# X, B and C of an SSD layer as pairs of seven block products ahead of the scan, a decay matrix by one exponential and a predicated copy, and what is left of the filler tiles behind

## The chip, the cores and the metric

The kernel runs on one core of one Trainium2 chip. The metric is the device time of one execution in microseconds (us), the median of several runs.

## The reference

It is a two-layer encoder on a sequence of 1024 tokens with 1024 channels, all in float32. The change touches the first layer alone, whose core is this:

```
proj = x @ w_in
z, xbc, dt_raw, sc_bg, sc_cg, sc_h, sc_gate = split(proj)
xbc = silu(depthwise_conv4(xbc) + conv_b)
xs, bm, cm = split(xbc)                    # 16 heads of 64; 4 groups of B and C, 128 states each
y_a = ssd(xs, bm, cm, dt) + ssd(flipped)   # both directions, chunks of 128
y_a = rms_norm(y_a * silu(z))
y_b = sc_bg * conv3(sc_cg * sc_h) * silu(sc_gate)
out = concat([y_a, y_b]) @ w_out
```

In a chunk of the scan, with cs the running sum of dt*a:

```
cb     = einsum('bclgn,bcsgn->bcgls', cq, bq)
y_diag = einsum('bcgls,bcgrls,bcsgrp->bclgrp', cb, exp(masked difference of cs), xd)
states = einsum('bclgn,bcgrl,bclgrp->bcgrpn', bq, decay_states, xd)
y_off  = einsum('bclgn,bcgrpn,bcgrl->bclgrp', cq, h_in, exp(cs))
```

Then follows a layer norm, and a second layer with latent attention and pooling.

## The kernel before

Every weight and x is split into a high and a low part in fp32r, and each product is three matmuls (high by high, high by low, low by high). A weight tile is loaded by SyncE (SP) as 512 KB into a raw buffer (wraw, three of them), cast by ScalarE to whi, and VectorE makes wlo as the difference. An output tile of 128 channels by 1024 tokens (key X, B, C or br, PSUM tile gps, of which there are two) has 8 steps of 6 matmuls of 128x512. PSUM also has four tiles of 512 columns (pool pb) for all small products.

A function main_plan writes the order of the work as a list, and a scheduler with pools of buffers fixes each engine's order from it:

- z of group 0 (zdp, evicted as zx) and the time steps dt, then the tiles B, C, X0, X1 of group 0.
- For each of four groups g a second pass (op_p2: a chunk's transposes xps, its scaled xd, its states sps; for later groups z tiles beside them), then a third pass over 8 chunks. Its front part (op_p3f) makes cbp = B'C and the decay matrix E: both directions of a row of cs come from DRAM by a broadcast transfer (E2 from crow, four buffers), VectorE adds a mask of -1e30, ScalarE takes 8 exponentials with a bias eb for each head and direction, VectorE adds the two halves and multiplies by cbp. Its back part (op_p3b) makes yo (from the states) and yd (E by x), and VectorE, GpSimd and ScalarE gather them as ta and yg; yg goes to DRAM (yad).
- In each chunk of a third pass stand F3 = 6 steps of filler tiles: the 16 br tiles of the short convolution and the X, B, C tiles of the next group. br tiles come in fours: q=1 is copied (bru), q=2 multiplied by it and convolved (bra), q=0 multiplied in, q=3 is the gate, after which the tile is stored (ybd).
- Behind the scan, four tiles of combinations of x are made (op_tp: xtraw loaded, differences, split to xT), and the other 16 br tiles go as 8 pairs, each by seven block products of 12 matmuls (sA, sB, sD; op_sw prepares the weight combinations from sraw, op_sp does a product).

A wrapper named issue_after places the mask add of a third pass behind the second pass's sixth xd. Four buffers of E2 mean that a chunk's transfer waits for the yd four chunks earlier.

Of the kernel before, what the change touches and what calls it, by code (L numbers as in the profile page):

```python
# [18 lines left out]
P = 128  # L19
# [12 lines left out]
NEG = np.float32(-1e30)  # L32
# [32 lines left out]
F2, F3, FB, FC = 0, 6, 4, 0  # L65
J0 = 4
# [11 lines left out]
def main_plan():  # L78
# [6 lines left out]
    def to_front(keys):  # L85
        n = 0
        while n < len(queue) and queue[n][2] != 0:
            n += 1
        queue[n:n] = [s for key in keys for s in tile_steps(key)]

# [4 lines left out]
    for key in (("B", 0), ("C", 0), ("X", 0), ("X", 1)):  # L95
        queue += tile_steps(key)
    ops.append(("dt",))
    pull(len(queue))
    for j in range(J0):
        for q in BR_ORDER:  # L100
            queue += tile_steps(("br", q, j))
    for g in range(G):
        ops.append(("z0", g))
        pull(FB)
        for i, c in enumerate(C2):
# [3 lines left out]
            pull(F2)  # L109
# [9 lines left out]
        pull(FC)  # L119
        for i, c in enumerate(C3):  # L120
# [6 lines left out]
            pull(F3)  # L127
            ops.append(("p3b", g, c))
        while any(s[1][0] in ("B", "C", "X") for s in queue):
            pull(1)  # L130
# [5 lines left out]
    ops += [("sw", 0, i) for i in range(SW_N)]  # L136
    pull(len(queue))
    ops.append(("sw", 1, 0))
    for n in range(NP):
        for i in range(7):  # L140
            ops.append(("sp", n, i))
            if n + 1 < NP and 0 < i + 1 < SW_N:
                ops.append(("sw", n + 1, i + 1))
        if n + 2 < NP:
            ops.append(("sw", n + 2, 0))
        if n in YA_P:
            ops.append(("ya", YA_P.index(n)))
# [4 lines left out]

SW_N = 6
YA_P = (1, 2)
PAIRS = [p for j in range(J0, 8) for p in ((("br", 1, j), ("br", 2, j)), (("br", 3, j), ("br", 0, j)))]
# [28 lines left out]
def pack(inputs):  # L184
# [17 lines left out]
    consts = np.concatenate([ident, up, up.T, NEG * (1 - up), NEG * (1 - up.T)], axis=1)  # L202
# [47 lines left out]
class Weights:  # L250
    def __init__(self, k, pool, ahead=1):
        self.k, self.pool, self.ahead = k, pool, ahead
        self.seq, self.idx = weight_seq(), weight_index()
        self.limit = self.seq.index(("O", 0))
        self.loaded = self.done = self.used = 0
        self.raw, self.out = {}, {}
# [24 lines left out]
    def release(self):  # L281
        self.limit = len(self.seq)
        self.split(self.used + 1 + self.ahead)
# [13 lines left out]
def setup(k):  # L297
# [4 lines left out]
    cs = k.const.tile([P, 640], F32, name="consts")  # L302
    k.ident, k.up, k.lo = (cs[:, 128 * i:128 * i + 128] for i in range(3))
    k.mask = view(cs[:, 384:640], 2)
# [114 lines left out]
def dt_chain(k, tp, X):  # L419
    nc, a, sp = k.nc, k.a, k.dts_pool  # L420
    V = nc.vector
    alog = tp.tile([P, 32], F32, name="alog")
    nc.sync.dma_start(out=alog, in_=a["alog"].partition_broadcast(P))
    dsk = tp.tile([P, 32], F32, name="dsk")
# [18 lines left out]
    dt = t("dt")  # L443
    V.scalar_tensor_tensor(out=dt, in0=p, scalar=2.0, in1=X, op0=ALU.mult, op1=ALU.add)
    da = t("da")
    V.scalar_tensor_tensor(out=view(da, NB), in0=view(dt, NB), scalar=-1.0, in1=bc_mid(aexp, 1, NB), op0=ALU.mult, op1=ALU.mult)
    ones = tp.tile([P, P], F32, name="ones")
# [11 lines left out]
    k.eb = sp.tile([P, 256], F32, name="eb")  # L459
# [3 lines left out]
    dec = t("dec")  # L463
    V.tensor_tensor(out=dec, in0=cp[:, 256:512], in1=k.cs, op=ALU.subtract)
    nc.scalar.activation(out=dec, in_=dec, func=AF.Exp)
    V.tensor_scalar(out=dt, in0=dt, scalar1=0.25, scalar2=None, op0=ALU.mult)
    V.tensor_tensor(out=k.dw, in0=dec, in1=dt, op=ALU.mult)
    V.tensor_scalar(out=dt, in0=dt, scalar1=1e-37, scalar2=None, op0=ALU.max)
    nc.scalar.activation(out=dt, in_=dt, func=AF.Ln)
    V.tensor_tensor(out=k.eb, in0=dt, in1=k.cs, op=ALU.subtract)  # L470
    k.crow = k.dram.tile([NB, 2, 16 * P], F32, name="crow")
    rowT = big(k, "rowT").bitcast(F32)[:32, 0:NB * P].rearrange("p (c l) -> p c l", c=NB)
# [17 lines left out]
def layer0_main(k):  # L490
# [1077 lines left out]
```

## Time and profile before

| | |
|---|---|
| runs | 1423.72, 1423.87, 1426.09 us (median 1423.87) |
| profiled execution | 1426.95 us |
| its span | 1424.8 us |
| mean granted clock of TensorE | 0.997 |

The three runs and the profiled execution are of the same kernel; a span goes from the first to the last instruction. The first filler matmul (gps) starts at 35.06 us, the gate pairs at 555.33, and the output projection of the first layer at 712.40.

### The profile page before, as it was taken

How to read it: one execution, taken by the hardware profiler on the slowest of the kernel's cores; microseconds unless marked ns; L12 is line 12 of the kernel's file. 1: busy time of each engine (PE TensorE's matmuls, PEld its weight loads, DVE VectorE, ACT ScalarE, POOL GpSimd, SP SyncE). 2: the span in 40 equal slices, each digit the busy share in tenths (PEclk: the TensorE clock that was granted, in tenths of full speed). 3: DMA queues.
4: the chain of work that ended last, by engine and by line, in shares of the span. 5: the costliest groups of instructions: out<-in, count | busy, mean ns of one | idle time of the engine just before them, and what ended most of it. 6: DMA issues, size and time to landing. Idle time of an engine off the chain costs nothing.

```text
span 1424.8 us, 19565 instructions
## 1 busy us (share of the span) xinstructions
PE 1394.6 (98%) x7287; PEld 1187.2 (83%) x7287; DVE 931.3 (65%) x1512; ACT 655.7 (46%) x1301; POOL 478.7 (34%) x443
## 2 busy tenths in 40 slices
PE   8999999999999999999999999999999999999997
PEld 8887798888889787788888888898888888988886
DVE  5758858839965947866564543733327888888485
ACT  5446545537536423433243422522225888878410
POOL 0013635423733543433210430612310445546210
PEclk9999999999999999999999999999999999999999
DMA  7221523421430524232268355211100000001232
GB/s 253 69 72 45 119 75 91 109 82 32 144 114 10 150 82 140 80 95 74 85 196 274 104 159 192 81 32 45 44 23 1 1 1 1 1 31 60 89 118 89
DMA packets 47726, 123.39 MB, mean 87 GB/s; under 512 B 5512, under 2 KB 10384, under 8 KB 47632
## 3 DMA queue, kind: packets, MB, share of 16 engines
q1 hardware_dynamic: 47632, 122.14, 27.8%
q8 instruction: 58, 0.95, 0.3%
q14 instruction: 36, 0.29, 0.1%
HBM read 105.21 MB, written 16.91 MB: 86 GB/s over the span
## 4 chain that ended last, share of the span: by engine, by line
PE 79%; DVE 10%; DMA 3%; ACT 3%; issue 2%; POOL 2%; DVEq 0%; SPq 0%; ACTq 0%; POOLq 0%
PE sA L907 6%; PE gps L409 5%; PE gps L410 5%; PE gps L412 5%; PE ops L412 4%; PE ops L410 4%; PE ops L409 4%; PE tps L1390 3%; PE fps L404 3%; PE fps L402 3%; PE fps L403 3%; PE sD L907 3%; PE sps L402 2%; PE sps L403 2%; PE sps L404 2%
## 5 line engine op out<-in xcount | busy, mean ns | idle before, releaser
L409 PE MATMUL gps<-x,whi 128*128 128x512 f32 x512 | 206.2, 403 | 3.6 <-DVE cacc L593 3.0
L410 PE MATMUL gps<-x,whi 128*128 128x512 f32 x512 | 202.3, 395 | 0.0
L412 PE MATMUL gps<-x,wlo 128*128 128x512 f32 x512 | 162.8, 396 | 0.1
L484 DVE TENSOR_TENSOR wlo<-wraw,whi 128x1024 fp32r<-128x1024 f32 x66 | 85.4, 1297 | 76.7 <-ACT whi L483 76.5
L483 ACT CAST whi<-wraw 128x1024 fp32r<-128x1024 f32 x66 | 69.0, 1049 | 122.7 <-PE ops L412 38.6
L409 PEld LDWEIGHTS gps<-x,whi 128*128 128x128 f32 x512 | 96.7, 189 | 26.4 <-issue 3.1
L412 PEld LDWEIGHTS gps<-x,wlo 128*128 128x128 f32 x512 | 95.7, 189 | 21.2 <-issue 1.2
L410 PEld LDWEIGHTS gps<-x,whi 128*128 128x128 f32 x512 | 96.7, 189 | 19.7 <-issue 1.2
L1376 POOL TENSOR_SCALAR pt<-pt,sm 128x1024 f32<-128x1024 f32 x64 | 72.8, 1138 | 114.3 <-DVE sm L1375 63.3
L484 POOL TENSOR_TENSOR xdl<-xd,xdh 128x512 fp32r<-128x512 f32 (+1 forms) x32 | 40.2, 1256 | 178.7 <-ACT xdh L483 175.3
L484 DVE TENSOR_TENSOR PT<-tps,PT 128x512 fp32r<-128x512 f32 x128 | 84.1, 682 | 14.2 <-ACT PT L483 14.0
L771 ACT ACTIVATE E<-E,eb 128x128 f32<-128x128 f32 x256 | 78.4, 391 | 25.3 <-DVE E L768 17.9
L1370 DVE TENSOR_REDUCE nm<-sps 128x1 f32<-128x1024 f32 x64 | 77.9, 1218 | 9.5 <-PE sps L404 9.3
L987 POOL TENSOR_TENSOR rs<-rs,neghalf 128x1 f32<-128x1 f32 x16 | 12.9, 811 | 210.5 <-DVE nm L1022 142.8
L1374 ACT ACTIVATE pt<-sps,nm 128x1024 f32<-128x1024 f32 x64 | 71.8, 1122 | 17.4 <-DVE nm L1371 12.6
L483 ACT CAST PT<-tps 128x512 fp32r<-128x512 f32 x128 | 70.0, 588 | 17.2 <-PE tps L1390 16.6
L795 POOL TENSOR_TENSOR ta<-to,ta 128x256 f32<-128x256 f32 x56 | 57.5, 1027 | 53.0 <-DVE to L788 50.1
L402 PE MATMUL fps<-x1hi,whi 128*128 128x512 f32 x192 | 74.9, 390 | 0.0
L404 PE MATMUL fps<-x1hi,wlo 128*128 128x512 f32 x192 | 74.7, 389 | 0.0
L403 PE MATMUL fps<-x1lo,whi 128*128 128x512 f32 x192 | 74.7, 389 | 0.0
L593 DVE SCALAR_TENSOR_TENSOR cacc<-gps,vec,cacc 128x512 f32<-128x512 f32 (+1 forms) x96 | 71.5, 745 | 2.4 <-ACT cacc L589 1.4
L1390 PE MATMUL tps<-consts,pt 128*128 128x128 f32 x512 | 70.9, 274 | 0.6 <-DVE PT L484 0.3
(372 smaller groups left out, 3823.9 us busy)
## 6 DMA issues: line engine op xcount, KB each, us to landing
wraw<-in_wt_dram SPq DMA_DIRECT2D x82, 512.0 KB, 4.3
E<-crow SPq DMA_DIRECT2D x32, 512.0 KB, 5.6
sraw<-in_wt_dram SPq DMA_DIRECT2D x16, 512.0 KB, 4.3
yad<-yg SPq DMA_DIRECT2D x32, 128.0 KB, 2.2
ybd<-bra SPq DMA_DIRECT2D x16, 256.0 KB, 2.4
xtraw<-in_xT_dram SPq DMA_DIRECT2D x8, 512.0 KB, 3.8
yab<-yad SPq DMA_DIRECT2D x8, 512.0 KB, 3.5
ybr<-ybd SPq DMA_DIRECT2D x8, 512.0 KB, 4.4
```

Source lines behind the costliest of these rows:

```text
L402: nc.tensor.matmul(out, shi, mhi, start=start, stop=False)
L403: nc.tensor.matmul(out, shi, mlo, start=False, stop=False)
L404: nc.tensor.matmul(out, slo, mhi, start=False, stop=stop)
L409: nc.tensor.matmul(out, shi, mhi, start=start, stop=False)
L410: nc.tensor.matmul(out, shi, mlo, start=False, stop=False)
L412: nc.tensor.matmul(out, slo, mhi, start=False, stop=stop)
L483: nc.scalar.copy(out=hi, in_=src)
L484: lo_eng.tensor_tensor(out=lo, in0=src, in1=hi.bitcast(F32), op=ALU.subtract)
L771: A.activation(out=E4[:, d, h], in_=E4[:, d, h], func=AF.Exp, bias=eb4[:, c, d, 4 * g + h:4 * g + h + 1])
L907: PE.matmul(ps, s_[:, kk, :], x_, start=fresh and kk == 0 and m == 0, stop=kk == 3 and m == 2, skip_group_check=True)
L1370: V.tensor_reduce(out=nm, in_=ps, axis=AX.X, op=ALU.max)
L1390: PE.transpose(out=ps[:, P * c:P * c + P], in_=pt[:, P * (4 * h + c):P * (4 * h + c) + P], identity=k.ident)
```

## The change

- X, B and C are no filler tiles any more. They become 8 pairs, (B, C) and (X, X) of each group, by the same seven block products as the gate pairs, all ahead of the scan. Each result is convolved over 1024 columns at a time, with one Silu, stored to DRAM (xbd), and loaded again for its group by op_xl.
- The combinations xT are made in front, under the first 4 br tiles, and again behind for the gate pairs. z of group 0 goes by DRAM too (z0d).
- The other 12 br tiles (96 steps) are the filler: 8 steps ahead of the scan, 1 a chunk in group 0's second pass, and 3, 2, 2 and 3 a chunk in the third passes.
- The decay matrix: the backward half gets a bias of ed (the difference of the two biases), a mask is copied into PSUM, a predicated copy puts the backward half over the forward one, and then there is one set of four exponentials. What both directions count on the diagonal goes into cd, which takes dsum's place in ta.

```diff
-F2, F3, FB, FC = 0, 6, 4, 0
-J0 = 4
+F2, F3, FB, FX = (1, 0, 0, 0), (3, 2, 2, 3), 0, 8
+JF, J0 = 1, 4
...
+    per = len(queue) // 4
+    for t in range(4):
+        pull(per // 2)
+        ops.append(("tp", t))
+        if t == 3:
+            ops.append(("sw", 0, 0))
+        pull(per - per // 2)
+    pull(len(queue))
+    ops += [("sw", 0, i) for i in range(1, SW_N)]
+    ops.append(("sw", 1, 0))
+    ops.append(("dt",))
+    pairs(0, NF, SW_FRONT, {})
+    for j in range(JF, J0):
+        for q in BR_ORDER:
+            queue += tile_steps(("br", q, j))
+    ops.append(("ssd",))
+    pull(FX)
...
         if g + 1 < G:
-            to_front([("X", 2 * g + 2), ("X", 2 * g + 3), ("B", g + 1), ("C", g + 1)])
+            ops.append(("xl", g + 1))
...
+PAIRS = [p for g in range(G) for p in ((("B", g), ("C", g)), (("X", 2 * g), ("X", 2 * g + 1)))]
+NF = len(PAIRS)
...
+    def op_xl(g):
+        groups[g]["xfm"] = view(big(k, "xfm").bitcast(F32), 4)
+        for j in (2, 3, 0, 1):
+            nc.sync.dma_start(out=groups[g]["xfm"][:, j], in_=k.xbd[g, :, j])
...
+        acc = acc4("cacc")
+        A.activation(out=acc, in_=u, func=AF.Identity, bias=k.vec[:, V_CONVB + idx:V_CONVB + idx + 1], scale=w(2))
+        for i, sh in ((1, -1), (0, -2), (3, 1)):
+            a0, a1 = max(-sh, 0), S - max(sh, 0)
+            V.scalar_tensor_tensor(out=acc[:, a0:a1], in0=u[:, a0 + sh:a1 + sh], scalar=w(i), in1=acc[:, a0:a1], op0=ALU.mult, op1=ALU.add)
+        A.activation(out=acc, in_=acc, func=AF.Silu)
+        nc.sync.dma_start(out=k.xbd[g, :, j], in_=acc)
...
         with tc.issue_after(st["xd", C2[E_AT]]):
-            V.tensor_tensor(out=E4, in0=E4, in1=bc_mid(k.mask, 2, HPG), op=ALU.add)
+            for h in range(HPG):
+                A.activation(out=E4[:, 1, h], in_=E4[:, 1, h], func=AF.Identity, bias=ed4[:, c, 4 * g + h:4 * g + h + 1])
+            A.copy(out=later, in_=k.mask)
+            V.copy_predicated(out=E, mask=bc_mid(later.bitcast(I32), 1, HPG), data=E4[:, 1])
         for h in range(HPG):
-            for d in range(2):
-                A.activation(out=E4[:, d, h], in_=E4[:, d, h], func=AF.Exp, bias=eb4[:, c, d, 4 * g + h:4 * g + h + 1])
-        V.tensor_tensor(out=E, in0=E, in1=tb, op=ALU.add)
-        V.tensor_tensor(out=view(E, HPG), in0=view(E, HPG), in1=bc_mid(cbp, 1, HPG), op=ALU.mult)
+            A.activation(out=E[:, h], in_=E[:, h], func=AF.Exp, bias=eb4[:, c, 0, 4 * g + h:4 * g + h + 1])
+        cd = tp.tile([P, 8], F32, name="cd", tag="cd", bufs=3)
+        junk = tp.tile([P, P], F32, name="junk", tag="junk", bufs=1)
+        V.scalar_tensor_tensor(out=junk, in0=cb, scalar=1.0, in1=k.ident, op0=ALU.mult, op1=ALU.mult, accum_out=cd[:, 4:5])
+        V.scalar_tensor_tensor(out=cd[:, 0:4], in0=dt4[:, c, 1, g4], scalar=cd[:, 4:5], in1=k.dsum[:, g4], op0=ALU.mult, op1=ALU.add)
+        V.tensor_tensor(out=E, in0=E, in1=bc_mid(cb, 1, HPG), op=ALU.mult)
```

What this does to the order shows at three places. First VectorE at the start, with L859 the differences of op_tp, L573 and L577 the evictions of dt and z; in the kernel after:

```order
L495 TENSOR_TENSOR wlo_424<-wraw_376,whi_423 128x1024
L495 TENSOR_TENSOR wlo_494<-wraw_427,whi_493 128x1024
L859 TENSOR_TENSOR xtraw_454<-xtraw_454 128x512
L859 TENSOR_TENSOR xtraw_454<-xtraw_455,xtraw_454 128x512
L859 TENSOR_TENSOR xtraw_455<-xtraw_455,xtraw_454 128x512
L859 TENSOR_TENSOR xtraw_455<-xtraw_455 128x512
L495 TENSOR_TENSOR xT4_462<-xtraw_454,xT4_462 128x1024
L573 TENSOR_TENSOR dtx_380<-zdp_96,dtb_381 128x64
L573 TENSOR_TENSOR dtx_380<-zdp_97,dtb_381 128x64
L495 TENSOR_TENSOR xT4_462<-xtraw_455,xT4_462 128x1024
```

Before, the evictions (there L562 and L565) follow the two weight splits at once; now a tile of combinations stands between them.

Second, ScalarE at the end of group 1's third pass, in the kernel after. L794 is the addition of ed, L798 the exponentials, L831 the squares of a finished chunk; E2_3398 and E2_3447 belong to the last two chunks of group 1, E2_4018, E2_4037 and E2_4093 to the first three of group 2:

```order
L794 ACTIVATE E2_3447<-E2_3447,ed_786 128x128 x4
L795 COPY cbp_3396<-consts_63 128x128
L794 ACTIVATE E2_4018<-E2_4018,ed_786 128x128 x4
L798 ACTIVATE E2_3398<-E2_3398,dtx_380 128x128 x4
L795 COPY cbp_3445<-consts_63 128x128
L831 ACTIVATE ta_3387,ssq_67<-yg_3392 128x256
L794 ACTIVATE E2_4037<-E2_4037,ed_786 128x128 x4
L798 ACTIVATE E2_3447<-E2_3447,dtx_380 128x128 x4
L831 ACTIVATE ta_3436,ssq_67<-yg_3441 128x256
L794 ACTIVATE E2_4093<-E2_4093,ed_786 128x128 x4
```

The additions for group 2 stand between those of group 1 and its exponentials. In the kernel before, what first touches the next group's E2 (E2_2107 to E2_2291 of group 1) is VectorE's mask add, behind that group's sixth xd:

```order
L712 TENSOR_TENSOR xd_1938<-xps_1930,dw_448 128x512
L768 TENSOR_TENSOR E2_2107<-E2_2107,consts_63 128x1024
L768 TENSOR_TENSOR E2_2122<-E2_2122,consts_63 128x1024
L768 TENSOR_TENSOR E2_2198<-E2_2198,consts_63 128x1024
L768 TENSOR_TENSOR E2_2291<-E2_2291,consts_63 128x1024
```

The first touch of a new group's E2 has moved to another engine and from behind the second pass to ahead of the last exponentials of the group before.

Third, TensorE between the scan and the gate pairs, in the kernel after:

```order
L425 MATMUL gps_5212<-x01_91,wlo_5047 128x512
L425 MATMUL gps_5212<-x11_93,wlo_5047 128x512
L817 MATMUL yo_5280<-hin_4445,xfm_4011 128x256
L823 MATMUL yd_5284<-zx_4432,E2_5187 128x64 x4
L817 MATMUL yo_5338<-hin_4445,xfm_4011 128x256
L823 MATMUL yd_5342<-zx_4432,E2_5245 128x64 x4
L841 MATMUL rinvp_5360<-consts_63,rinv_5355 8x128
L939 MATMUL sA_5427<-x00_90,whi_5403 128x512 x2
L939 MATMUL sA_5427<-x00_90,wlo_5404 128x512
```

Before, the last yd (yd_5058) is followed by two whole filler tiles, gps_5106 and gps_5194, 96 matmuls, ahead of the first sA; now nothing of that kind is left there.

## Rows read from the trace of the kernel before

**Rows 1.** The page: span, then busy us, share and instructions of each engine.

```profile
span 1424.8 us, 19565 instructions
PE 1394.6 (98%) x7287; PEld 1187.2 (83%) x7287; DVE 931.3 (65%) x1512; ACT 655.7 (46%) x1301; POOL 478.7 (34%) x443
```

**Rows 2.** Table by stretches: busy us of each engine, clock, DMA share, GB/s.

```profile
134.30:186.50 52.20, 50.25 (x249) 40.05 (x248) 45.32 (x67) 24.04 (x64) 33.67 (x37) 1.00 0.56 127
...
555.30:712.40 157.10, 154.10 (x692) 126.71 (x691) 103.06 (x107) 56.87 (x78) 51.96 (x35) 1.00 0.28 88
```

**Rows 3.** Timeline of TensorE ahead of the gate pairs: start, duration, instruction.

```profile
552.84 0.39 PE L410 MATMUL gps<-x,whi 128*128 128x512 f32 x1
...
555.33 0.62 PE L907 MATMUL sA<-x,whi 128*128 128x512 f32 x2
```

**Rows 4.** Groups of VectorE instructions by line, 0 to 560 us: busy us, mean ns.

```profile
L768 DVE TENSOR_TENSOR E<-E,consts 128x1024 f32<-128x1024 f32 x32 | 47.7, 1519 | 4.9 <-DMA E<-crow 4.8
...
L772 DVE TENSOR_TENSOR E<-E 128x512 f32<-128x512 f32 x32 | 23.6, 737 | 10.4 <-ACT E L771 10.3
...
L827 DVE TENSOR_TENSOR xtraw<-xtraw 128x512 f32<-128x512 f32 x16 | 11.4, 714 | 6.8 <-DMA xtraw<-in_xT_dram 6.7
...
L484 DVE TENSOR_TENSOR xT<-xtraw,xT 128x1024 fp32r<-128x1024 f32 x8 | 10.1, 1270 | 0.0
```

**Rows 5.** Timelines of VectorE and TensorE at the start.

```profile
28.98 1.23 DVE L484 TENSOR_TENSOR wlo<-wraw,whi 128x1024 fp32r<-128x1024 f32 x1 [1.07 <-ACT whi L483]
...
33.80 0.68 DVE L565 SCALAR_TENSOR_TENSOR zx<-zt,zdp 128x512 f32<-128x512 f32 x1
...
35.06 0.40 PE L409 MATMUL gps<-x,whi 128*128 128x512 f32 x1
```

**Rows 6.** The page's transfers: line of issue, count, KB each, median us to landing.

```profile
wraw<-in_wt_dram SPq DMA_DIRECT2D x82, 512.0 KB, 4.3
...
xtraw<-in_xT_dram SPq DMA_DIRECT2D x8, 512.0 KB, 3.8
```

**Rows 7.** Timeline of ScalarE in a third pass: eight exponentials in one row.

```profile
255.81 2.45 ACT L771 ACTIVATE E<-E,eb 128x128 f32<-128x128 f32 x8 [2.05 <-DVE E L768]
```

**Rows 8.** E's transfer (L765): its waiter, its landing, and SP's waits.

```profile
  DVE E L768: 4.8, 6
...
DMA to landing us min/median/max: 4.7/5.6/13.2
...
SPq L765 <- PE yd L791: 23.6, 8, 5.7
```

**Rows 9.** The chain that ended last, around 237 us: start, us, what.

```profile
236.64 0.86 PE yo L785 x2
237.50 0.84 PE yd L791 x8
238.37 4.81 DMA E<-crow
```

**Rows 10.** The chain near 544 us, and TensorE's waits in the first pair.

```profile
543.97 3.82 DMA xtraw<-in_xT_dram
...
551.62 5.34 DMA sraw<-in_wt_dram
...
566.65 0.50 PE L907 MATMUL sA<-x,wlo 128*128 128x512 f32 x1 [1.55 <-DVE wlo L484]
575.39 0.73 PE L907 MATMUL sA<-xT,whi 128*128 128x512 f32 x2 [1.20 <-ACT snap L871]
```

**Rows 11.** TensorE after a gap, then stretches with the granted clock behind POOL.

```profile
121.85 0.62 PE L409 MATMUL gps<-x,whi 128*128 128x512 f32 x1 [2.15 <-DVE cacc L593]
...
122.00:124.00 2.00, 2.00 (x6) 1.53 (x7) 1.76 (x5) 2.00 (x5) 0.00 (x0) 0.52 0.03 8
124.00:126.00 2.00, 2.00 (x7) 1.63 (x6) 2.00 (x3) 1.82 (x4) 1.61 (x1) 0.63 0.00 0
...
564.00:568.00 4.00, 2.19 (x9) 1.43 (x9) 4.00 (x4) 0.32 (x1) 0.38 (x1) 1.00 0.50 161
```

More of the change, by code (lines that the diff above doesn't have):

```diff
@@ L1 @@
-from contextlib import ExitStack
+from contextlib import ExitStack, nullcontext
 import numpy as np
@@ L83, in tile_steps @@
         return [("fm", key, kk) for kk in range(KD)]
[L85 to L89, printed above, removed]
     def pull(n):
@@ L93, in pull, with pairs @@
             ops.append(queue.pop(0))
[L95 to L99, printed above, removed]
+    def pairs(first, count, sched, final):
+        for n in range(first, first + count):
+            for i in range(7):
+                ops.append(("sp", n, i))
+                if n + 1 < first + count:
+                    ops.extend(("sw", n + 1, m) for m in sched.get(i, ()))
+            if n + 2 < first + count:
+                ops.append(("sw", n + 2, 0))
+            ops.extend(final.get(n, ()))
+    for j in range(JF):
         for q in BR_ORDER:
             queue += tile_steps(("br", q, j))
+    ops.append(("zx",))
+    per = len(queue) // 4
[15 more added lines that the diff above has]
+    pull(FX)
     for g in range(G):
@@ L135, in main_plan @@
     pull(4)
-    ops += [("sw", 0, i) for i in range(SW_N)]
+    ops += [("sw", NF, i) for i in range(SW_N)]
     pull(len(queue))
[L138 to L147, printed above, removed]
+    ops.append(("sw", NF + 1, 0))
+    pairs(NF, NP - NF, SW_BACK, {NF + n: [("ya", i)] for i, n in enumerate(YA_P)})
     for c in range(len(YA_P), NB):
@@ L281, in release @@
     def release(self):
-        self.limit = len(self.seq)
-        self.split(self.used + 1 + self.ahead)
+        self.limit = self.limits.pop(0)
+        self.split(self.used + 1)
     def get(self, key):
@@ L577, in cv @@
     def cv(name):
-        return cvp.tile([P, 512], F32, name=name, tag="cv", bufs=CVB)
+        return (fp or cvp).tile([P, 512], F32, name=name, tag="cv", bufs=2 if fp is not None else CVB)
     def t1(name, dt=F32):
@@ new lines, in fm_finish @@
+        q, j = key[1], key[2]
+        hs = [slice(0, HALF), slice(HALF, S)]
+        if q == 1:
+            br["u"] = t4("bru")
+            A.copy(out=br["u"], in_=ps)
+        elif q == 2:
+            u = br["u"]
+            V.tensor_tensor(out=u, in0=ps, in1=u, op=ALU.mult)
+            br_conv(u, j)
+        elif q == 0:
+            for h in range(2):
+                V.tensor_tensor(out=br["a"][h], in0=ps[:, hs[h]], in1=br["a"][h], op=ALU.mult)
+        else:
+            for h in range(2):
+                th = cv("brt")
+                A.activation(out=th, in_=ps[:, hs[h]], func=AF.Tanh, scale=0.5)
+                V.scalar_tensor_tensor(out=th, in0=th, scalar=1.0, in1=ps[:, hs[h]], op0=ALU.add, op1=ALU.mult)
+                acc = br["a"][h]
+                GP.tensor_tensor(out=acc, in0=acc, in1=th, op=ALU.mult)
+                nc.sync.dma_start(out=k.ybd[j, :, hs[h]], in_=acc)
@@ L655, in layer0_main, with op_hold @@
     live = {}
+    hold = None
+    def op_hold(g):
+        nonlocal hold
+        hold = None if g is None else groups[g]["xp"]
     def op_fm(key, kk):
@@ L661, in op_fm @@
         wh, wl = view(whi, KD), view(wlo, KD)
-        mm6(nc, halves(ps), wh[:, kk, :], wl[:, kk, :], *zip(*(xhl(h, kk) for h in range(2))), kk == 0, kk == KD - 1)
+        with tc.issue_after(hold) if hold is not None and kk == 0 else nullcontext():
+            mm6(nc, halves(ps), wh[:, kk, :], wl[:, kk, :], *zip(*(xhl(h, kk) for h in range(2))), kk == 0, kk == KD - 1)
         if kk == KD - 1:
@@ L759, in op_p3f @@
         blk = slice(P * c, P * c + P)
-        cbp = k.pb.tile([P, 512], F32, name="cbp", tag="pb")[:, 0:P]
-        PE.matmul(cbp, st["xfm"][:, 2, blk], st["xfm"][:, 3, blk], start=True, stop=True)
+        cbp = k.pb.tile([P, 512], F32, name="cbp", tag="pb")
+        cb, later = cbp[:, 0:P], cbp[:, P:2 * P]
+        PE.matmul(cb, st["xfm"][:, 2, blk], st["xfm"][:, 3, blk], start=True, stop=True)
         E2 = tp.tile([P, 2, 512], F32, name="E2", tag="E2", bufs=E2B)
-        E, tb = E2[:, 0], E2[:, 1]
         hs = slice(512 * g, 512 * g + 512)
@@ L945, in op_sp @@
             W.release()
+            W.split(W.used + 1 + W.ahead)
     k.ay = {}
```

209 lines of the change are left out of this document (103 added, 106 removed).

## The prediction

> **What bounds the kernel now.** I read the page first: TensorE is busy for 1394.6 of 1424.8 us, VectorE for 65% of it, and no other engine for half [rows 1]. So time comes off in two ways only: fewer matmul columns, or fewer waits of TensorE. The table by stretches then shows how little there is of the second between the first filler tile and the output projection: 50.25 of 52.20 us are busy in group 0's third pass, 154.10 of 157.10 in the gate pairs [rows 2]. A busy figure overlaps with its neighbours, so I took the price of a 128x512 matmul from two starts: from 552.84 to 555.33 us stand 11 of them, 0.2264 us each [rows 3]. Adding such prices row by row in TensorE's order (an estimate, since the order has no times) gives 656.3 us of work from 35.06 to 712.40 us, 677.3 us: some 21 us are lost there before, in small pieces. The filler tiles, 6 steps of 6 matmuls (8.2 us) a chunk, are what hides every chain of transfers and of elementwise work. I therefore asked of each edit what it takes from that filler, and what then shows.
>
> **The change part by part.**
>
> *Products.* 16 tiles of 8 steps of 6 matmuls become 8 pairs of 7 products of 12: 8 x (96 - 84) = 96 matmuls fewer, 96 x 0.2264 = **-21.7 us** [rows 3]. This is certain, as the order has them; everything else is what it costs to collect it. VectorE and ScalarE get some 14 and 9 us of work in a pair of 19 us (added up from rows such as 4), so neither bounds the pairs by its amount.
>
> *Start.* Before, the z evictions free the PSUM tiles by 34.5 us and the first filler matmul starts at 35.06 [rows 5]. Now VectorE has the differences of two xT tiles and the split of the first ahead of the first z eviction (first order piece). The second xT tile takes the raw buffer that the split at 28.98 frees at 30.2 [rows 5]; with a landing of 3.8 to 4.3 us it is there by some 34.5 [rows 6]. Behind it stand three differences (0.71 each, 2.1), two splits (1.27 each, 2.5), four small sums (0.5) and the eviction of 0.68: about 40.3 [rows 4, 5]. **+5.3**; 0 if the transfer lands far earlier, 7 if it is delayed by the others in flight.
>
> *Pairs, dt chain and reload.* The X, B, C results go to DRAM and come back in 512 KB pieces. Group 0's tile needs a buffer that the last product frees, and the transposes need three pieces of it, which were issued one behind the other at about 4 us each [rows 6]; the cover is 8 steps, 10.9 us, less what the last products still run. **+3**, from 0 (the cover is enough) to 8 (no cover counts).
>
> *Group 0's second pass.* Its cover falls from whole tiles to a step per chunk, and a filler tile's multiply stands ahead of a chunk's xd on VectorE. **+2** (0 to 5), by that one 1024-wide multiply twice, at about the 1.27 of a 1024-wide difference [rows 4].
>
> *Decay matrix.* Before, a chunk takes a mask add (1.52 us), 8 exponentials (2.45 us) and an add (0.74) [rows 4, 7]; now 4 ScalarE additions of the same shape (half of 2.45: 1.22), a mask copy, a predicated copy, 4 exponentials (1.22) and two small sums. The predicated copy has no row; I bound it by a 512-wide difference (0.71) and the 1024-wide mask add (1.52), and take 0.74, the add of its own width [rows 4]. The work in all falls by 1 to 2 us a chunk on VectorE; since TensorE waits for latency, that by itself is worth nothing. What matters is order. Before, VectorE met the next group's mask add only behind that group's sixth xd. Now ScalarE meets the next group's addition ahead of *this* group's last exponentials (second order piece), and that addition waits for a transfer which waits for a buffer. In group 1: the buffer is freed by yd of the fifth chunk, the transfer lands 4.7 us later at the least and 5.6 in the median [rows 8] (4.81 in the chain that ended last, started by such a yd [rows 9]), then 1.22 for the addition, 1.22 for the exponentials, 0.7 for the multiply of 512 [rows 4, 7]: 7.8 to 8.7 us before the seventh yd. TensorE's order has no filler left there: a yo and a yd (0.86 + 0.84), another yo of half that and two cbp, 2.4 in all [rows 9]. So 5.4 to 6.3 us show, and the next chunk repeats it with what is left, 0 to 2. Its second-pass evictions stand behind two more such additions, up to 2.5. By the same arithmetic group 0 shows 4.6 to 7.2, group 2 4.9 to 8.8, and group 1 5.4 to 10.9: 14.9 to 26.9 together. I take 22, nearer the top, because the queue of SP already waits for yd here [rows 8]. Before, these three ends lost 7.0 by the sum of prices, of which the first shows 1.95 as idle [rows 2]. **+15** (+8 to +20; -7 if none of it shows).
>
> *End of the SSD.* Before, 96 filler matmuls, 21.8 us, stand between the last yd and the first product of the gate pairs. Now the queue is empty (third order piece). Under them ran the chain of transfers: xT 3.82, then a weight tile 5.34, and the pairs still waited 1.55 and 1.20 [rows 10]. Now the second xT transfer stands in SP's queue behind the store of the last gated filler tile, and the weight tile behind the store of a yg: the issue comes some 4.7 us after the last filler matmul, the landing 4.9 later, the cast 1.07 as VectorE waited for one at the start [rows 5]: 10.6, where yo and yd fill 2.5. With the later splits that is 10.7 against some 3 before (those two and small ones). **+8** (5 to 10).
>
> *Clock.* After the gap of 2.15 us before 121.85 the granted clock was 0.52 and 0.63 in the next 4 us, which cost 2 x 0.48 + 2 x 0.37 = 1.7 us; after the gap of 1.55 us it stayed at 1.00 [rows 10, 11]. Of the new gaps some three are longer than that: 3 x 1.7 = **+5** (0 to 12). The Trainium skill, page "TensorE: Matmul & The Clock Gate", section "HAM oscillation — how this bites in real kernels", says that an array which is starved again and again between short bursts falls to its slow clock each time and begins every burst there. By that rule all nine or so new gaps would pay, 15 us in place of 5; the row of 2.15 us agrees, the row of 1.55 does not.
>
> Sum: -21.7 + 5.3 + 3 + 2 + 15 + 8 + 5 = **+16.6**. The profiled execution took 1426.95 us, so 1443.6 for one; the median of the runs is 3.1 below it, so **1440.5**.
>
> **The rivals.** *Faster: the ends of the third passes cost nothing.* If the transfers for the next group land before ScalarE comes to its additions, the decay term is -7, and with the clock at 2 the sum is -21.7 + 5.3 + 3 + 2 - 7 + 8 + 2 = -8.4: 1415.5. For it: VectorE waited for these transfers only 4.8 us in all before [rows 8]. Against it: there it had 8.2 us of filler a chunk. It decides once all new stalls together stay under 21.7 us; with none at all the time is 1402. *VectorE binds in the pairs:* one operation of a 1024-wide convolution (1.3 us) ahead of a pair's last split, 8 times, is 10 us more: 1451. Against it: 14 of 19 us busy. *Every gap pays the clock:* the nine or so new gaps (one or two at each of three ends, the start, the reload, the end) at 1.7 us each are 15 in place of 5, so 1450.5; the gap of 1.55 us that cost nothing speaks against it [rows 10, 11]. *The change gives no products* is excluded by the order. A price of 1.5 for the predicated copy adds 0.8 to each of three tails, inside the bounds.
>
> **How the numbers follow.** My forecast 0.50, ends that cost nothing 0.27, VectorE in the pairs 0.08, the clock at every gap 0.09, and 0.06 for stalls that just cancel the gain (with the forecast's low edge the 0.08 below). The likeliest case alone: the bounds of its terms not all at one end, 1426 to 1458. Against the products stands a sum of stalls none of which I could see running, so the range goes down to the faster rival and below, **1408 to 1458**. A difference under 0.2% (2.8 us) can't be told from none here: faster 0.28, same 0.08, slower 0.64.
>
> **What would show each step.** TensorE has 96 fewer 512-wide matmuls. The first filler matmul starts near 40 us in place of 35. At the end of groups 0, 1 and 2 yd waits for VectorE's multiply, and behind it the ScalarE additions wait for E from crow, 5 us or more. Between the last yd and the first sA lies a gap of 8 us. The granted clock falls behind the long gaps. I am wrong above all if the ends of the third passes show gaps under 2 us, or if ScalarE's additions find their data landed.

## The result and the profile after

The changed kernel takes 1485.12 us in the median (1484.23 to 1485.86, 4 runs) against 1423.85: ratio 1.0423, 95% interval 1.0403 to 1.0442. It is slower by 61 us where 16.6 were forecast, and lies far outside the range. The 96 matmuls are gone, and almost four times their worth (80 us against 21.7) was lost elsewhere.

The page of the changed kernel, the lines that answer to [rows 1], and the granted clock in 40 slices of the span:

```profile
span 1483.2 us, 19661 instructions
PE 1394.1 (94%) x7191; PEld 1184.5 (80%) x7191; DVE 941.9 (64%) x1576; ACT 700.5 (47%) x1359; POOL 476.4 (32%) x459
...
PEclk9999999798989899799999999999999999999999
```

TensorE has 96 instructions fewer and yet the same busy time: what the products saved, matmuls at a lower clock took back. All dents of the clock lie in the first 17 slices, up to the gate pairs. The table by stretches gives each stage: start up to the pairs, the front pairs, then second and third pass of groups 0 to 3 by turns (the last with the scan's end), then the gate pairs. Columns: length, busy us of TensorE (count), of its weight loads, VectorE, ScalarE, GpSimd, granted clock, share of the DMA engines, GB/s.

```profile
40.17:89.53 49.36, 47.33 (x206) 38.83 (x207) 38.36 (x59) 19.43 (x27) 5.72 (x4) 0.96 0.41 125
89.53:253.81 164.28, 164.28 (x723) 135.28 (x721) 126.56 (x119) 82.25 (x99) 28.67 (x15) 1.00 0.34 121
253.81:299.17 45.36, 32.65 (x139) 25.26 (x138) 18.87 (x31) 20.99 (x54) 12.83 (x15) 0.81 0.58 154
299.17:347.17 48.00, 40.20 (x201) 31.98 (x199) 30.45 (x69) 29.37 (x89) 27.90 (x37) 0.94 0.53 140
347.17:380.87 33.70, 33.65 (x246) 32.28 (x247) 12.36 (x29) 16.59 (x46) 12.79 (x14) 0.94 0.23 83
380.87:426.99 46.12, 39.88 (x188) 31.44 (x187) 34.66 (x75) 25.75 (x82) 25.14 (x36) 0.88 0.55 138
426.99:470.08 43.09, 37.06 (x246) 34.19 (x247) 24.78 (x72) 20.80 (x56) 13.58 (x15) 0.89 0.25 74
470.08:514.61 44.53, 39.49 (x189) 31.41 (x187) 31.08 (x71) 26.40 (x83) 27.11 (x36) 0.89 0.54 150
514.61:548.85 34.24, 33.89 (x247) 32.31 (x248) 12.40 (x29) 17.93 (x52) 14.33 (x17) 0.94 0.16 36
548.85:617.58 68.73, 48.23 (x237) 38.37 (x235) 57.23 (x103) 31.83 (x87) 38.40 (x42) 0.88 0.45 130
617.58:772.65 155.07, 155.07 (x694) 128.27 (x694) 99.19 (x105) 56.54 (x77) 48.38 (x32) 0.99 0.27 84
```

The pairs in front are busy throughout at full clock, and the gate pairs behind too. Between them, in the scan, no other engine is busy for more than 83% of a stage (VectorE in the last one), and TensorE idles in almost every stage. Compare the first line of [rows 2]: the third pass of group 0 had 1.95 us idle then and has 7.80 now. The timeline of TensorE names the waits; these are the larger ones of 24 (start, duration, instruction, idle time ahead and what ended it):

```profile
40.17 0.77 PE L422 MATMUL gps<-x,whi 128*128 128x512 f32 x1 [6.33 <-DVE dtx L573]
...
273.92 0.58 PE L415 MATMUL sps<-xdh,bhl 128*128 128x256 f32 x1 [6.05 <-ACT xdh L494]
...
280.92 0.80 PE L415 MATMUL sps<-xdh,bhl 128*128 128x512 f32 x1 [5.36 <-ACT xdh L494]
...
345.43 1.94 PE L823 MATMUL yd<-zx,E 128*128 128x64 f32 x8 [6.78 <-issue]
...
451.74 0.79 PE L415 MATMUL sps<-xdh,bhl 128*128 128x512 f32 x1 [3.76 <-ACT xdh L494]
...
617.58 0.37 PE L841 MATMUL rinvp<-consts,rinv 128*8 128x128 f32 x1 [16.02 <-DVE rinv L839]
```

I added up all of them up to 772.65 us, without the very first wait for data, which both kernels have: 66.8 us, against 8.3 before. The second loss is the clock. In stretches of 2 us each, TensorE's busy time times one minus the granted clock adds up to 23.2 us over the first 800 us, against 1.7 before. One such place is the end of group 0's third pass, in stretches of 2 us:

```profile
342.00:344.00 2.00, 0.00 (x0) 0.00 (x0) 0.76 (x5) 2.00 (x9) 1.20 (x2) 0.50 0.40 158
344.00:346.00 2.00, 0.57 (x3) 0.60 (x4) 0.69 (x1) 1.45 (x6) 0.86 (x2) 0.50 0.95 357
346.00:348.00 2.00, 2.00 (x11) 2.00 (x11) 0.42 (x1) 0.84 (x4) 0.01 (x1) 0.50 0.09 33
348.00:350.00 2.00, 2.00 (x12) 2.00 (x11) 0.62 (x2) 1.46 (x5) 0.95 (x2) 0.50 0.42 137
350.00:352.00 2.00, 2.00 (x14) 2.00 (x14) 0.00 (x0) 0.00 (x0) 0.49 (x1) 0.67 0.66 174
```

After the wait of 6.78 us TensorE runs at 0.50, the lower of its two levels (1.2 GHz), and it is back only some 5 us later: 2.9 us in all by the same sum. The books close: 58.5 us of idle time, 21.5 of clock, -21.7 of products make 58.3, and the spans differ by 58.4. (The medians differ by 61.3, since the profiled execution of the kernel before was 3.1 us above its median.)

### The profile page after: what moved, and what is told of

The parts are those of the page before. It is cut to its first block, busy times and chain, and to the rows that moved or that the text cites. A ratio compares the mean times of both kernels' runs of the same rounds, so it can differ in the third digit from the quotient of the medians.

```text
span 1483.2 us, 19661 instructions
## 1 busy us (share of the span) xinstructions
PE 1394.1 (94%) x7191; PEld 1184.5 (80%) x7191; DVE 941.9 (64%) x1576; ACT 700.5 (47%) x1359; POOL 476.4 (32%) x459
## 4 chain that ended last, share of the span: by engine, by line
PE 79%; DMA 7%; DVE 6%; ACT 3%; issue 3%; POOL 1%; SPq 0%; DVEq 0%; ACTq 0%; POOLq 0%
PE sA L939 12%; PE sD L939 6%; DMA E<-crow 5%; PE ops L423 4%; PE ops L425 4%; PE ops L422 4%; PE tps L1445 3%; PE fps L416 3%; PE sB L939 3%; PE fps L415 3%; PE fps L417 3%; PE gps L422 2%; PE gps L423 2%; PE sps L415 2%; PE gps L425 2%
## 5 line engine op out<-in xcount | busy, mean ns | idle before, releaser
L422 PE MATMUL gps<-x,whi 128*128 128x512 f32 x256 | 104.8, 409 | 6.3 <-DVE dtx L573 6.3
L495 DVE TENSOR_TENSOR wlo<-wraw,whi 128x1024 fp32r<-128x1024 f32 x50 | 64.9, 1299 | 65.4 <-ACT whi L494 65.3
L423 PE MATMUL gps<-x,whi 128*128 128x512 f32 x256 | 104.8, 410 | 0.0
L888 POOL TENSOR_TENSOR s3t<-sraw 128x512 f32<-128x512 f32 x16 | 27.5, 1722 | 226.8 <-DMA sraw<-in_wt_dram 172.5
L494 ACT CAST whi<-wraw 128x1024 fp32r<-128x1024 f32 x50 | 52.3, 1049 | 94.7 <-PE ops L425 39.2
L495 DVE TENSOR_TENSOR PT<-tps,PT 128x512 fp32r<-128x512 f32 x128 | 84.2, 682 | 12.6 <-ACT PT L494 12.3
L425 PE MATMUL gps<-x,wlo 128*128 128x512 f32 x256 | 86.9, 410 | 0.0
L794 ACT ACTIVATE E<-E,ed 128x128 f32<-128x128 f32 x128 | 41.2, 390 | 57.4 <-DMA E<-crow 54.5
L629 DVE SCALAR_TENSOR_TENSOR cacc<-u,vec,cacc 128x1023 f32<-128x1023 f32 (+1 forms) x48 | 66.8, 1407 | 1.5 <-ACT cacc L626 1.3
L1460 PE MATMUL yps<-PT,vv 128*128 128x256 f32 x256 | 65.7, 286 | 0.0
L1445 PEld LDWEIGHTS tps<-consts,pt 128*128 128x128 f32 x512 | 59.7, 141 | 7.2 <-DVE PT L495 1.1
L494 ACT CAST whi<-sraw 128x1024 fp32r<-128x1024 f32 x40 | 41.2, 1049 | 50.4 <-PE sD L939 40.9
```

The costliest lines, as they stand in the source:

```text
L422: nc.tensor.matmul(out, shi, mhi, start=start, stop=False)
L423: nc.tensor.matmul(out, shi, mlo, start=False, stop=False)
L425: nc.tensor.matmul(out, slo, mhi, start=False, stop=stop)
L494: nc.scalar.copy(out=hi, in_=src)
L495: lo_eng.tensor_tensor(out=lo, in0=src, in1=hi.bitcast(F32), op=ALU.subtract)
L1445: PE.transpose(out=ps[:, P * c:P * c + P], in_=pt[:, P * (4 * h + c):P * (4 * h + c) + P], identity=k.ident)
```

## The experiments

Sixteen kernels ran. Those of the first table are the changed kernel with something undone or altered; those of the second are the kernel before with parts of the change. Each ratio is to the kernel before on the same chip, where its median lay between 1422.38 and 1425.89 us; between chips, compare the ratios.

| changed kernel, with | us | ratio (95%) |
|---|---|---|
| nothing else | 1485.12 | 1.0423 (1.0403 to 1.0442) |
| ScalarE's additions held | 1484.86 | 1.0425 (1.0409 to 1.0440) |
| old decay matrix | 1490.52 | 1.0468 (1.0441 to 1.0496) |
| every reload twice | 1492.10 | 1.0474 (1.0452 to 1.0496) |
| rinv later | 1485.87 | 1.0424 (1.0401 to 1.0447) |
| 20 filler tiles | 1462.86 | 1.0273 (1.0257 to 1.0288) |
| 20 filler tiles, held | 1448.49 | 1.0172 (1.0157 to 1.0187) |
| 20 filler tiles, held, 16 steps at the end | 1437.68 | 1.0104 (1.0083 to 1.0126) |
| the same, z evictions first | 1439.54 | 1.0097 (1.0078 to 1.0116) |
| 16 filler tiles, held, 16 steps at the end | 1458.60 | 1.0244 (1.0219 to 1.0269) |

| kernel before, with | us | ratio (95%) |
|---|---|---|
| new decay matrix as in the change | 1424.19 | 0.9990 (0.9979 to 1.0001) |
| new decay matrix, held | 1418.61 | 0.9958 (0.9941 to 0.9974) |
| the same, 5 steps a chunk, 2 more pairs | 1411.63 | 0.9905 (0.9888 to 0.9923) |
| the same, 4 steps a chunk, 4 more pairs | 1432.48 | 1.0062 (1.0041 to 1.0082) |
| the same, 3 steps a chunk, 6 more pairs | 1455.26 | 1.0224 (1.0206 to 1.0241) |
| 4 steps, 4 more pairs, no filler ahead of the second passes | 1445.26 | 1.0159 (1.0142 to 1.0176) |
| old decay matrix, 3 steps a chunk, same work | 1442.78 | 1.0118 (1.0097 to 1.0139) |

### The order on ScalarE

My prediction's largest term rested on ScalarE meeting the additions of ed too early. The wrapper issue_after holds only what stands on the engine of the instruction that it names; with the additions on ScalarE and the xd on VectorE it holds the predicated copy alone, as the second order piece shows. The first run holds the additions too:

```diff
-        split(nc, xh[:, cols], xl[:, cols], xd[:, cols], nc.gpsimd)
+        st["xh", c] = A.copy(out=xh[:, cols], in_=xd[:, cols]).ins
+        GP.tensor_tensor(out=xl[:, cols], in0=xd[:, cols], in1=xh[:, cols].bitcast(F32), op=ALU.subtract)
...
-        with tc.issue_after(st["xd", C2[E_AT]]):
+        with tc.issue_after(st["xh", C2[E_AT]]):
             for h in range(HPG):
                 A.activation(out=E4[:, 1, h], ...
             A.copy(out=later, in_=k.mask)
+        with tc.issue_after(st["xd", C2[E_AT]]):
             V.copy_predicated(...)
```

> The changed kernel with ScalarE's additions and mask copies of a group placed behind that group's sixth xdh cast (the predicated copy stays behind the sixth xd). Theory A (ScalarE meets the additions of E too early and waits there for the transfer, and with it the casts and exponentials that TensorE needs): the waits of the second passes of groups 0 and 2 and of the ends of groups 0 to 2 go, some 30 of the 59 us of new idle time and two thirds of the 21 us lost to the lower clock: 1440 us (1432 to 1452). Theory B (the filler is too thin for the chain of a chunk, whatever the order on ScalarE): within 10 us of 1485. Theory C (the reloads of X, B, C delay E's transfers): within 10 us of 1485 too.

> The changed kernel with the decay matrix of before (VectorE's mask add, held behind the sixth xd, and eight exponentials), the rest as changed. Theory A: the same gain as the held additions, 1442 us (1434 to 1455), since what matters is the order. Theory B: within 10 us of 1485. If this lies 10 us or more above the held version, the old chain's longer latency counts under thin filler.

> The kernel before with the new decay matrix alone, written as in the change (additions not held on ScalarE); filler, X, B, C and the end as before. Theory A: slower than before even under full filler, by the waits of the second passes: 1436 us (1430 to 1450). Theory B: the thick filler hides it, 1424 us (within 4). Theory C: as B, since nothing is reloaded.

> The kernel before with the new decay matrix, additions held on ScalarE behind the sixth xdh cast. All theories: 1424 us (1420 to 1428), since TensorE there hides the chain; A needs it clearly under the run without the hold.

Held, the changed kernel takes 1484.86 us: no gain. With the decay matrix of before (and its hold on VectorE) it takes 1490.52, where theory A had 1442. So theory A, that the order on ScalarE is what the 61 us come from, fell. What the hold did is to move the loss: TensorE's idle time fell by 10.6 us, from 66.8 to 56.2, of which 8.0 lie in group 0's second pass (12.6 to 4.6), and the lower clock took 11.2 back. TensorE's waits in the held run, grouped by what they wait for (us in total, times, longest):

```profile
PE rinvp L843 <- DVE rinv L841: 10.6, 1, 10.6
PE yd L825 <- issue: 8.5, 3, 4.5
...
PE yo L819 <- DVE to L822: 5.5, 4, 2.1
PE sps L415 <- ACT xdh L738: 5.4, 3, 3.8
```

The waits of sps for the cast xdh fell from 16.2 us to 5.4, and rinv's from 16.0 to 10.6, but yo and yd now wait in more places, and the sum over the clock went from 23.2 to 34.4 us. The end of group 1, first as changed, then held (columns as above):

```profile
400.00:430.00 30.00, 23.76 (x113) 19.36 (x112) 18.86 (x44) 17.36 (x60) 15.17 (x22) 0.77 0.59 155
```

```profile
400.00:430.00 30.00, 20.39 (x91) 15.93 (x90) 16.15 (x40) 14.72 (x51) 15.82 (x22) 0.74 0.57 135
```

On the kernel before, with 6 steps of filler a chunk, the new decay matrix costs nothing even without the hold (1424.19, where theory A had 1436). There the same hold is worth 5.6 us (1424.19 to 1418.61; their intervals, up to 0.9974 and from 0.9979, just do not touch); 1418.61 lies below the 1420 to 1428 us expected. Held and fully covered, the new decay matrix is 0.4% faster than the old one. So the edit to the decay matrix is sound, and the hold is worth something only where other waits do not take its place.

### The reloads

```diff
         for j in (2, 3, 0, 1):
-            nc.sync.dma_start(out=groups[g]["xfm"][:, j], in_=k.xbd[g, :, j])
+            for _ in range(2):
+                nc.sync.dma_start(out=groups[g]["xfm"][:, j], in_=k.xbd[g, :, j])
```

> The changed kernel with every reload of X, B, C issued twice into the same place (2 MB more a group). Theory C: another 8 to 20 us on top, 1495 to 1505. Theory B: the second passes' first transposes of group 0 may wait, but the rest is as before: 1485 to 1490 us.

1492.10 us: 7 us in the median for 8 MB more (3.3 us in the profiled executions). In that profile sps waits 5.3 us for a weight tile, in group 0's second pass, where it had waited for none; yet the idle time in all is 65.4 us against 66.8, and it is the sum over the clock that is higher, 27.3 against 23.2. The time lies between the two expectations. If a second reload costs about what the first one does, which no run without reloads tests, 7 us are far from 61.

### The filler

```diff
-F2, F3, FB, FX = (1, 0, 0, 0), (3, 2, 2, 3), 0, 8
-JF, J0 = 1, 4
+F2, F3, FB, FX = (1, 0, 0, 0), (5, 4, 4, 5), 0, 8
+JF, J0 = 1, 6
```

> The changed kernel with 20 filler tiles in the scan in place of 12 (J0 = 6; 5, 4, 4 and 5 steps a chunk in the third passes) and 4 gate pairs in place of 8: 48 matmuls more, 10.9 us. Theory B (the filler is too thin for the chain of a chunk): at nearly the 6 steps of before the waits and the lower clock lose half of their 80 us or more: 1456 us (1440 to 1468). Theory C (the reloads and stores of X, B, C slow E's transfers): the traffic is the same, 1496 us (1488 to 1500). The old theory A (order on ScalarE): 1490 us or more.

> As the run with 20 filler tiles, with ScalarE's additions held behind the sixth xdh cast. Theory B alone: equal to the run without the hold (within 5 us). Theory A and B together (the order counts once the filler covers the rest, as it did under the full filler of before, 6 us): 6 to 15 us less than without the hold, 1446 us (1435 to 1455).

> As the run with 20 filler tiles and the hold, with 4 steps a chunk in each third pass, so that 16 steps (21.8 us) are left behind the last yd as before. If the end's wait (16 us of which rinv is the last link) is a matter of cover: 10 to 15 us less than the run before it minus what the thinner groups 0 and 3 cost (0 to 5): 1436 us (1428 to 1448). If rinv's chain is what ends last whatever lies there: within 3 us of it.

The second adds the hold, the third has (4, 4, 4, 4), so that 16 steps are left for the end. The first, 1462.86, fell into the range of theory B, that the filler is too thin, at unchanged traffic, where theory C had 1488 or more; the second, 1448.49, into that of A and B together, where B alone had no gain from the hold; the third, 1437.68, into that of an end without cover. Each has 48 matmuls (10.9 us) more than the changed kernel, and yet it gains 22, 37 and 47 us. Now the hold is worth 14.4 us, and the waits that it removes are those it was meant for; first without it, then held:

```profile
PE sps L415 <- ACT xdh L494: 19.4, 8, 5.8
PE rinvp L841 <- DVE rinv L839: 11.5, 1, 11.5
```

```profile
PE rinvp L843 <- DVE rinv L841: 11.4, 1, 11.4
...
PE sps L415 <- ACT xdh L738: 5.4, 3, 3.8
```

With 16 steps behind the scan the wait for rinv is gone from the list altogether: 10.8 us less, with groups 0 and 3 thinned from 5 steps to 4. Of that last version's 24.4 us of idle time (before the output projection, without the first wait) 6.7 are the start's, 2.0 the time steps', 5.1 group 0's second pass, 5.8 group 2's; no yo or yd waits in any third pass. The next run thins them again, with (3, 3, 3, 3) and J0 = 5, the end being kept:

> As the changed kernel with the hold and 16 steps kept for the end, with 16 filler tiles, 3 steps a chunk, in place of 20 and 4: 24 matmuls fewer, 5.4 us. If 3 steps cover the third pass with the new decay matrix: 1432 us (1429 to 1435). If cover runs out between 4 and 3: 1440 to 1460.

1458.60 us: 21 us more, although 24 matmuls (5.4 us) are gone. yo and yd wait again, the idle time in all goes from 24.4 to 34.5 us, and the sum over the clock from 5.8 to 17.7, most of it in groups 0 to 2:

```profile
PE yo L819 <- DVE to L822: 2.5, 3, 1.3
...
PE yd L825 <- issue: 1.7, 1, 1.7
```

The same on the kernel before, where nothing of X, B, C is moved. First its third passes thinned at equal work and equal traffic:

```diff
-F2, F3, FB, FC = 0, 6, 4, 0
+F2, F3, FB, FC = 0, 3, 4, 0
```

> The kernel before with 3 steps of filler a chunk in the third passes in place of 6; the rest of the X, B, C tiles is pulled at each third pass's end, the rest of the br tiles behind the scan, so that work and traffic are the same. Theory B (the cover alone decides): the third passes lose 5 to 10 us each and the lower clock follows: 1452 us (1440 to 1470). Theory C or any cost of the pairs, the reloads or the new decay matrix: within 5 us of 1424.

1442.78 us, 17 us lost without one matmul more or less (7287 in both), by the order alone: the profile has 15 us more idle time and 4 more of clock, 7.3 of the idle time ahead of the first sA, where TensorE waits for the cast of the pairs' first weights. Then the versions with the new decay matrix held, where filler tiles become gate pairs (J0 = 3, 2, 1) and F3 falls to 5, 4, 3:

> The kernel before with the new decay matrix held, 12 br tiles as filler in place of 16, 5 steps a chunk in the third passes in place of 6, 16 steps left for the end, and 10 gate pairs: 24 matmuls fewer, 5.4 us. If 5 steps still cover a chunk: 1413 us (1411 to 1416). If cover is already short at 5: 1418 to 1428.

> As the 5-step version of before, with 8 br tiles as filler, 4 steps a chunk and 12 gate pairs: another 24 matmuls fewer, 5.4 us. If 4 steps still cover a chunk, as they did in the third passes of the run with 20 filler tiles: 1406 us (1404 to 1409). If cover runs out between 5 and 4: 1412 to 1425.

> The same with 4 br tiles as filler, 3 steps a chunk and 14 gate pairs: 10.9 us of products less than the 5-step version. If cover runs out between 4 and 3 steps: 1415 to 1435. If the 3 steps of the thinned kernel before cost only through the old decay matrix: 1402 to 1406.

At 5 steps the time is 1411.63 us (1411.02 to 1413.7, 5 runs), 0.9905 of before: it beats both kernels, with 24 matmuls fewer than the kernel before. TensorE's waits in it show why it could. Up to the output projection, and behind the very first, they are two of 1 us or more and three of 0.2 to 0.3, and the sum over the clock is 0.0:

```profile
PE sA L920 <- DVE wlo L486: 1.5, 1, 1.5
PE sA L920 <- ACT snap L884: 1.0, 1, 1.0
```

At 4 steps the time jumps to 1432.48, at 3 to 1455.26, each with another 5.4 us of products saved; both lie above either of their two expectations. The longest waits of TensorE at 4 steps, then at 3 (that of zdp is the very first one, for data):

```profile
PE sA L920 <- ACT whi L485: 10.1, 1, 10.1
PE zdp L402 <- ACT zdh L485: 7.0, 1, 7.0
PE yd L804 <- issue: 5.0, 2, 2.9
```

```profile
PE rinvp L822 <- DVE rinv L820: 17.3, 1, 17.3
PE zdp L402 <- ACT zdh L485: 7.8, 1, 7.8
PE yo L798 <- DVE E L784: 5.9, 5, 1.9
```

These two do not measure the third passes alone. The plan pulls what is left of the next group's tiles at each third pass's end, so that the filler is nearly used up behind the scan at 4 steps and already inside group 3 at 3. More than half of their new idle time is the empty end (11.3 of 18.3 us at 4 steps, 17.3 of 32.4 at 3). A run was to part the two, by keeping the 4 steps ahead of each second pass (FB = 0) for the end:

> As the 4-step version of before with 12 gate pairs, but the 4 steps ahead of each second pass are kept for the end, so that some 32 steps stand behind the third passes in place of 4. If the loss of the 4-step version is the empty end (its wait of 10 us ahead of the first sA): 1410 us (1405 to 1418). If 4 steps are too thin for the third passes: 1425 or more.

1445.26 us, worse than without. In its trace no filler stands between the last yd and the first sA; 98 of its matmuls follow behind that. So rinv was waited for 11.9 us and the first weights another 9.1, 21 us of idle time where 11 were: the run did not part the two, and the end again had no cover. What the traces do show of the third passes is that cbp, yo and yd wait 8.8 us in all at 4 steps and 10.3 in this run, against 0.2 at 5: in that kernel 4 steps did not quite cover a chunk. In the changed one, with 20 filler tiles, they did.

### The end and the start

```diff
-        PE.transpose(out=rp[:NB, 0:P], in_=r, identity=k.ident)
...
+    def op_rr():
+        rp = k.pb.tile([P, 512], F32, name="rinvp", tag="pb")
+        PE.transpose(out=rp[:NB, 0:P], in_=k.rinv, identity=k.ident)
...
                 ops.append(("sp", n, i))
+                if n == NF and i == 1:
+                    ops.append(("rr",))
```

> The changed kernel with the transpose of rinv (and what follows it to rrow) two products later in TensorE's order. If rinv's chain alone delays the first sA by the 4 us that its weights are ready sooner: 1480 us (1477 to 1483). If the weights' chain is as late: within 1.5 us of 1485.

1485.87 us: no difference that the runs show. In the profile the first sA starts 4.9 us sooner (612.81 against 617.70), now waiting 10.49 us for its own weight's cast, but from it to the output projection 157.8 us pass in place of 155.0: products at the lower clock, and a wait of 1.36 that had not been there. From the last yd on 2.8 us remain in the profile, which the median does not confirm.

```diff
-        for o, p, q in ((a0, a1, a0), (a1, b1, a1), (b1, b1, a0), (b0, b0, b1)):
-            V.tensor_tensor(out=o, in0=p, in1=q, op=ALU.subtract)
+        with tc.issue_after(k.zlast) if fp is not None and kk == 0 else nullcontext():
+            for o, p, q in ((a0, a1, a0), (a1, b1, a1), (b1, b1, a0), (b0, b0, b1)):
+                V.tensor_tensor(out=o, in0=p, in1=q, op=ALU.subtract)
```

> The run with 20 filler tiles, the hold and 16 steps at the end, with VectorE's differences of the first xT behind the z evictions. The first filler matmul then starts at 35 us as before, and the lower clock behind its gap goes: 5 to 8 us less than 1437.7, 1431 us (1429 to 1434). If the differences then come late for the first pair: 1435 or more.

1439.54 against 1437.68 us (ratios 1.0097 and 1.0104): no gain. The wait ahead of the first filler tile is gone from its timeline, but the same time is lost 50 us later, where the time steps' rows (rps) wait:

```profile
87.68 1.89 PE L487 MATMUL rps<-consts,cs 128*32 128x128 f32 x8 [8.62 <-ACT cs L471]
```

That was 2.02 us in the run without the edit. The front has 4 filler tiles for the chains of xT and of dt together, and what one of them gains the other loses.

## Why the prediction was wrong

Beside each term stands what the traces show for it, as idle time of TensorE after less before:

| term | forecast | measured |
|---|---|---|
| products | -21.7 | -21.7 |
| start | +5.3 | +6.3 |
| pairs, dt chain, reload | +3 | +2.0 |
| group 0's second pass | +2 | +10.5 |
| ends of the third passes | +15 | +22.9 |
| end of the scan | +8 | +16.7 |
| clock | +5 | +21.5 |
| sum | +16.6 | +58.2 |

The stalls were put at 38.3 us and came to 79.9. Four terms failed, the clock by most.

**Products, -21.7.** Right. TensorE has 7191 in place of 7287 instructions, and both sets of pairs run without idle time.

**Start, +5.3.** Right in its place and size: 40.17 against 35.06, by the wait for dtx of 6.33. As the run with the z evictions first shows, it is no loss of its own but a part of a front that is short of cover.

**Pairs, dt chain and reload, +3.** Right: 2.03 us of wait for cs, and by the sum of prices some 1.2 us of the pairs above that of their matmuls. The first transposes met their data.

**Group 0's second pass, +2.** Failed: 12.6 us of waits against 2.15 before. I saw the early additions in the third passes' ends and did not look for them in the first second pass, where the same order holds; with the additions held 4.6 us are left. The chain that ended last passes through there, with the slowest landing of all:

```profile
264.26 14.80 DMA E<-crow
...
279.09 1.28 ACT E L794 x4
280.37 0.52 ACT xdh L494
...
280.92 0.80 PE sps L415
```

E's first four transfers were issued together, and the cast that sps needs stood behind the additions. In the chain of [rows 9] such a transfer took 4.81 us, but that was a single one. In the kernel before the first four were issued together too, with one weight tile between them and no reload near, and the last of them took 13.2 us to land, the longest of [rows 8]. SP's timeline there, then in the changed kernel:

```profile
60.26 1.41 SPq L765 DMA_DIRECT2D E<-crow  x3
...
63.22 1.32 SPq L765 DMA_DIRECT2D E<-crow  x1
```

```profile
262.81 3.26 SPq L789 DMA_DIRECT2D E<-crow  x4
266.17 5.91 SPq L602 DMA_DIRECT2D xfm<-xbd  x4
```

So a landing of 13 to 15 us is not new. What is new is when it is waited for: before, VectorE's first use of E stood at 110.6 us, 47 us behind the last of these issues; now ScalarE's stands at 268.7, 6 us behind the first. The issue stood behind the landing of the last pair's store at 262.76, though the transfer that writes crow was issued at 90.5. Issuing these four earlier was not tried.

**Ends of the third passes, +15.** Mis-sized, and with a cause that does not decide. The places were nearly as forecast (6.78 us ahead of the last yd of group 0, 2.92 and 2.21 ahead of the seventh in groups 1 and 2), ScalarE's additions did wait for E's transfers (54.5 us in 29 waits), and with the second passes behind them the ends show 25.3 us against the 22 that I had taken. But I had then taken off 7.0 for what these ends lost before, from a sum of prices; the trace has 2.4 us of idle time there, so the term came to +22.9, above its range. Likewise the 21 us that I put down as lost before are 8.3 of idle time and 1.7 of clock. And the cause that I gave, the order on ScalarE, is not what decides here: with the additions held these stages lose 26.7 us, and the time stayed. Under 2 or 3 steps a chunk, TensorE's own work in a chunk is an estimated 4.6 to 6.0 us (those steps at 1.36 each, with some 1.9 for yo, yd and cbp by [rows 9]), and the chain of transfer, additions, predicated copy, exponentials and multiply does not fit under it in either order that ran. With 4 steps in the version with 20 filler tiles, and with 5 on the kernel before, it fits.

**End of the scan, +8.** Mis-sized: 20.5 us of waits against 3.8 before. I had priced the weights' chain only, at 8.1 ahead of the first sA and 10.7 with the later splits; the run with rinv later shows that chain at 10.49 and 11.85. What I left out is the third link of my own order piece: rinvp stands ahead of the first sA in TensorE's order, and rinv waits for the last squares, then for VectorE's xT work, then for GpSimd's power (2.57 us). The chain that ended last, near its end:

```profile
608.33 0.68 POOL yg L830
609.00 4.56 issue
613.57 0.04 POOLq L888
613.61 2.57 POOL rinv L838
...
616.20 1.24 DVE rinv L839
```

**Clock, +5.** The step that failed by most: 21.5 us. I took three gaps at 1.7 us, from the one gap of [rows 11] that cost something. Seven places paid, and each more than that. Single gaps cost 2.0 to 2.9 us, and the longest not the most (6.33 us cost 2.0, 6.78 cost 2.9, 16.02 cost 2.3), group 0's second pass 3.5, and the ends of groups 1 and 2 lost 4.8 and 5.0, since there TensorE waits again before it is back: from 418 to 428 us the clock stays at 0.50 through two waits. My rival "every gap pays", 15 us, was nearer. The rule of the Trainium skill, page "TensorE: Matmul & The Clock Gate", section "HAM oscillation — how this bites in real kernels", that short bursts between waits run at the slow clock again and again, agrees with these rows; I had weighed it against a single gap of 1.55 us and found it too dear.

**The rivals.** VectorE as the bound in the front pairs is excluded: busy for 126.56 of 164.28 us there, no wait of TensorE. The predicated copy takes 0.737 us (mean of 32), as taken. That the ends would cost nothing is excluded by their 25.3 us.

**What the terms had in common.** I costed each edit's stall at its own place, as if the next stage would have slack. In these runs there was little: a stall that was removed in one place came back in the next, as a wait or as lower clock. The three edits that gave nothing bear this out (the hold and rinv in the changed kernel, the z evictions in the version with 20 filler tiles). So do the steps that paid: more filler gave 22 us, then the hold 14, then filler kept for the end 11. Not settled is how the 61 us divide between the thin third passes, group 0's second pass and the end, because each pays for the others' waits by the clock.

## What to carry to other kernels

Work that fills the waits of the busiest engine is worth its own time until the waits show: count how many microseconds of it each chunk has, and keep that above the chunk's longest chain (here 5 steps, 6.8 us, were enough, 3 were not, and 4 were in one kernel of the two). Cheaper products belong only to the surplus beyond that, and some of it must be kept for places where nothing else runs, such as the end of the scan. When an operation moves to another engine, look whether what held its place in the order moved with it; and when several waits share one thin cover, mend or cover them together before judging any one of the edits.

## What the hardware showed that I had not expected

The lower clock costs a third as much as the waits themselves, 21.5 us beside 58.5, and not in proportion to them: the longest, 16.02 us, cost 2.3, and the end of group 1, whose three waits come to 6.24, cost 4.8. From 418 to 428 us TensorE was at half clock from one wait through the next, with only some 4 us between them. A broadcast transfer of 512 KB that lands in 5.5 us in the median took 14.8 as the last of four issued together, and 13.2 in the kernel before, where four were issued together as well. And 96 matmuls fewer left TensorE's busy time where it was (1394.1 against 1394.6 us), so that a busy share alone would have shown nothing of the saving.
